# A decoder trunk's first projection fed by quarters of x from two DMA queues, and its last norm taken by halves

## The chip, the cores and the metric

The kernel runs on one core of one Trainium2 chip. The metric is device time in microseconds (us) for one execution. Engines are named as in the profile: PE is TensorE, PEld its weight loads, DVE is VectorE, ACT ScalarE, POOL GpSimd, SP SyncE, which issues DMAs. A name with a q behind it (SPq) is that engine's instruction queue.

## What is computed

Two decoder layers over 256 tokens of width 1024, in float32, and a final norm:

```
def _layer(x, ...):
    proj = _rmsnorm(x, g_mix) @ w_in                       # 7244 columns
    (qa, ka, va, qb, kb, vb, fl, qc, kc, vc, qi, ki, wi, gl) = split(proj)
    br_a = stick_breaking_attention(qa, ka, va)
    br_b = forgetting_attention(qb, kb, vb, cumsum of log_sigmoid(fl + b_forget))
    br_c = indexed_sparse_attention(rope(qc), rope(kc), vc, rope(qi), rope(ki), wi, top 64)
    y = sum over b of sigmoid(gate_b) * (br_b @ w_branch[b])
    x = x + y @ w_out
    return x + square(relu(_rmsnorm(x, g_mlp) @ w_up)) @ w_down

def reference(x, ...):
    for layer in range(2): x = _layer(x, ...)
    return _rmsnorm(x, g_final)        # x * rsqrt(mean(x * x) + 1e-6) * g_final
```

## The kernel before

Every matrix product keeps float32 accuracy with three matmuls in a shorter format: each operand is held as a high and a low part, and `mm3` (L117) adds high x high (L119), high x low (L120) and low x high (L121). Weights come from memory as `raw` tiles, four row tiles of 128 rows at a time; `split` (L84) makes the high part on ACT (`whi`, L91) and the low part on DVE (`wlo`, L92). There are four `raw` buffers and four of each part.

`norm_in` (L157) brings x into the form that the projection needs. x is held as two row blocks (j) of 128 tokens and two halves (h) of 512 columns. For each pair of 128-column blocks its `part` transposes four 128x128 pieces on PE (`xtp`, L168), writes the high part on ACT (`xTh`, L173) and the low part on DVE (`xTl`, L174), scaled by the layer's gain `gT`. For each half it squares x on ACT with a running sum (L178). The factor of the norm (`rstd_of`, three steps on POOL, L185 to L188) is applied only when a product is evacuated.

The head of the kernel is the first layer's projection of 1100 columns: `stream_groups` (L207) takes two column groups together, 364 columns into banks `mm` and 368 into banks `at`. The order is row tiles 0 to 3 of the first group, 0 to 3 of the second, then 4 to 7 of each. A tile is two matmul triples, one for each row block. Each finished group is evacuated by ACT (`ct`, L239). A third group of 368 columns follows. Before it, SP loads x in three pieces (two of 128 x 512, then the second half as one), the gains, and four row tiles of the first group one by one; every DMA is issued by SP. A scheduler orders each engine's instructions by its own estimate of their times; only PE keeps the written order, and only in one later place.

The tail is the last layer's down projection into two halves of 512 columns (cg), the second half with row block 0 finished before row block 1. For each row block DVE adds the product to x (L713), ACT squares it with a running sum (L716), DVE multiplies by the final gain (L717), POOL makes the factor (L185, L186, L188), ACT and DVE rescale one half each (L723, L725), and SP issues each half (L724, L726).

Of the kernel before, what the change touches and what calls it, by code (L numbers as in the profile page):

```python
# [9 lines left out]
F32 = mybir.dt.float32  # L10
# [11 lines left out]
EPS = 1e-6  # L22
# [10 lines left out]
def trunk_kernel(ctx: ExitStack, tc: tile.TileContext, x, positions, g_mix, w_in, b_forget, w_branch,  # L33
# [25 lines left out]
    gload = const.tile([16, 128], F32, name="gload", tag="gload")  # L59

    def load_x(h):
        dma.dma_start(xh[h], AP(x, h * 512, [[D, 128], [128 * D, 2], [1, 512]]))
# [11 lines left out]
    def g_cols(src, c):  # L74
        p = at_tile("gps")
        pe.transpose(p[:, 0:16], src, ident[0:16, 0:16])
        dve.tensor_copy(gT[:, c:c + 16], p[:, 0:16])

    g_cols(gload, 0)
# [4 lines left out]
    def split(raw, k, n, steps=1):  # L84
# [4 lines left out]
        m = k // steps  # L89
        for i in range(0, k, m):  # L90
            act.activation(h3[:, i:i + m], raw[:, i:i + m], AF.Copy)  # L91
            dve.tensor_sub(l3[:, i:i + m], raw[:, i:i + m], h3[:, i:i + m].bitcast(F32))  # L92
        return h3, l3
# [5 lines left out]
    def w_rows(src, off, rs, k0, n, loads=1):  # L99

        raw = raw_tile(4, n)
        m = 4 // loads
        for i in range(0, 4, m):
            dma.dma_start(raw[:, i:i + m, :], AP(src, off + (k0 + i) * 128 * rs, [[rs, 128], [128 * rs, m], [1, n]]))
        r = []
        for q in range(2):
            h, l = split(raw[:, 2 * q:2 * q + 2, :], 2, n, 2 if loads == 4 and q == 0 else 1)
            r += [(h[:, i, :], l[:, i, :]) for i in range(2)]
        return r

# [46 lines left out]
    def norm_in(gcol, banks):  # L157
# [4 lines left out]
        def part(h):  # L162
            for kp in range(2):
# [5 lines left out]
                for i in range(2):  # L169
# [3 lines left out]
                    act.activation(hi, p[:, i * 256:i * 256 + 256], AF.Copy, scale=g)  # L173
                    dve.scalar_tensor_tensor(lo, p[:, i * 256:i * 256 + 256], g, hi.bitcast(F32),  # L174
                                             op0=OP.mult, op1=OP.subtract)
            for j in range(2):
# [38 lines left out]
    for layer in range(DEPTH):  # L215
        wi0 = layer * D * COLS
        if layer == 0:
            wfirst = w_rows(w_in, C0 + 736, COLS, 0, 364, loads=4)
            load_x(1)
            xt, ss, part = norm_in(0, (at_tile, pt_tile))  # L220
            part(0)
            part(1)
        rstd = rstd_of(ss)
        with tc.tile_pool(name=f"att{layer}", bufs=1, reuse_waits="tile") as att:
            work = att

            rp = at_tile("rp")
            for j in range(2):
                pe.transpose(rp[:, j * 128:j * 128 + 128], rstd[:, j:j + 1].to_broadcast([128, 128]), ident)
            rb = small.tile([128, 272], F32, name="rb", tag="rb", bufs=1)[:, 0:256]  # L230
            act.activation(rb, rp[:, 0:256], AF.Copy)

            rhalf = small.tile([128, 2], F32, name="rhalf", tag="rhalf", bufs=1)
            pool.tensor_scalar(rhalf, rstd, 0.5, 1.0, op0=OP.mult, op1=OP.mult)
# [6 lines left out]
            cgs = [(736, 364), (0, 368)]  # L241
            stream_groups(xt, 8, w_in, [(wi0 + C0 + c, n) for c, n in cgs], COLS,
                          done=lambda g, o: ct_done(*cgs[g], o), first=wfirst if layer == 0 else None)
            ct_done(368, 368, stream_tok(xt, 8, w_in, wi0 + C0 + 368, COLS, 368))

            if layer == 0:
                gload2 = const.tile([16, 128], F32, name="gload2", tag="gload")
                dma.dma_start(gload2, AP(g_mlp, 0, [[128, 16], [1, 128]]))
# [58 lines left out]
                g_cols(gload2, 16)  # L307
# [357 lines left out]
        with tc.tile_pool(name=f"mlp{layer}", bufs=1, reuse_waits="tile") as mlp:  # L665
# [38 lines left out]
            if last:  # L704
                gfb = mlp.tile([128, D], F32, name="gfb")
                dma.dma_start(gfb, AP(g_final, 0, [[0, 128], [1, D]]))
                ss = small.tile([128, 2, 2], F32, name="ss")
            else:
                xt, ss, part = norm_in(layer * 8 + 8, (at_tile, pt_tile))
            for cg in range(2):  # L710
                o = stream_tok(uT, 32, w_down, layer * DFF * D + cg * 512, D, 512, split_last=last and cg == 1)
                for j in range(2):
                    dve.scalar_tensor_tensor(xs[j][cg], o[j], r2[:, j:j + 1], xs[j][cg], op0=OP.mult, op1=OP.add)  # L713
                    if last:
                        junk = small.tile([128, 512], mybir.dt.bfloat16, name="junk", tag="junk", bufs=1)
                        act.activation(junk, xs[j][cg], AF.Square, accum_out=ss[:, j, cg:cg + 1])  # L716
                        dve.tensor_mul(xs[j][cg], xs[j][cg], gfb[:, cg * 512:cg * 512 + 512])  # L717
                if not last:
                    part(cg)
                for j in range(2):  # L720
                    if last and cg == 1:
                        rl = rstd_of(ss[:, j:j + 1, :])
                        act.activation(xs[j][1], xs[j][1], AF.Copy, scale=rl)  # L723
                        dma.dma_start(AP(out, j * 128 * D + 512, [[D, 128], [1, 512]]), xs[j][1])  # L724
# [25 lines left out]
```

## Time and profile before

| | us |
|---|---|
| median of three runs | 889.51 (888.76 to 890.77) |
| the profiled execution | 889.98 |
| its span, first to last instruction | 888.3 |
| PE busy | 873.0 (98%) |
| DVE busy | 621.6 (70%) |
| ACT busy | 531.1 (60%) |
| POOL busy | 113.9 (13%) |

The span is what the trace covers; the rest of an execution's time lies around it. Shares are of the whole span, so they don't tell where PE stands still. The chain that ended last gives 92% of the span to PE, 4% to DVE, and 1% each to ACT, DMA and issue.

### The profile page before, as it was taken

How to read it: one execution, taken by the hardware profiler on the slowest of the kernel's cores; microseconds unless marked ns; L12 is line 12 of the kernel's file. 1: busy time of each engine (PE TensorE's matmuls, PEld its weight loads, DVE VectorE, ACT ScalarE, POOL GpSimd, SP SyncE). 2: the span in 40 equal slices, each digit the busy share in tenths (PEclk: the TensorE clock that was granted, in tenths of full speed). 3: DMA queues.
4: the chain of work that ended last, by engine and by line, in shares of the span. 5: the costliest groups of instructions: out<-in, count | busy, mean ns of one | idle time of the engine just before them, and what ended most of it. 6: DMA issues, size and time to landing. Idle time of an engine off the chain costs nothing.

```text
span 888.3 us, 13911 instructions
## 1 busy us (share of the span) xinstructions
PE 873.0 (98%) x5342; PEld 789.1 (89%) x5342; DVE 621.6 (70%) x1008; ACT 531.1 (60%) x874; POOL 113.9 (13%) x216
## 2 busy tenths in 40 slices
PE   7999999999999999999999999999999999999996
PEld 7998998888889999888899989988888999998885
DVE  5899787978766666545468987789876676664552
ACT  6766886776455555444365758677755655553442
POOL 2300321234001000000011014022600100000001
PEclk9999999999999999999999999999999999999998
DMA  8744544354555555555466463453346555555521
GB/s 288 244 147 143 190 143 143 116 169 143 190 190 164 176 183 190 190 189 190 137 208 195 139 197 136 143 189 128 106 150 232 169 190 190 190 188 192 190 95 48
DMA packets 102482, 150.97 MB, mean 170 GB/s; under 512 B 2928, under 2 KB 58256, under 8 KB 102416
## 3 DMA queue, kind: packets, MB, share of 16 engines
q1 hardware_dynamic: 102416, 150.08, 51.5%
q8 instruction: 42, 0.69, 0.3%
q14 instruction: 24, 0.20, 0.1%
HBM read 149.02 MB, written 1.05 MB: 169 GB/s over the span
## 4 chain that ended last, share of the span: by engine, by line
PE 92%; DVE 4%; ACT 1%; DMA 1%; issue 1%; SPq 0%; POOL 0%; POOLq 0%; ACTq 0%
PE mm L120 26%; PE mm L119 26%; PE mm L121 26%; PE av L454 2%; PE pT L438 2%; PE at L120 1%; PE at L121 1%; PE at L119 1%; DVE wlo L92 1%; DVE qs L145 1%; PE xtp L168 1%; ACT qs L143 1%; DMA x<-in_x_dram 1%; PE za L347 0%; PE yTp L579 0%
## 5 line engine op out<-in xcount | busy, mean ns | idle before, releaser
L92 DVE TENSOR_TENSOR wlo<-raw,whi 128x1024 fp32r<-128x1024 f32 (+3 forms) x289 | 347.8, 1206 | 201.0 <-ACT whi L91 199.4
L91 ACT ACTIVATE whi<-raw 128x1024 fp32r<-128x1024 f32 (+3 forms) x289 | 298.5, 1036 | 253.1 <-PE mm L121 142.4
L121 PE MATMUL mm<-xTh,wlo 128*128 128x256 f32 x752 | 214.0, 285 | 0.0
L119 PE MATMUL mm<-xTh,whi 128*128 128x256 f32 x752 | 213.8, 284 | 0.0
L120 PE MATMUL mm<-xTl,whi 128*128 128x256 f32 x752 | 213.6, 284 | 0.0
L119 PEld LDWEIGHTS mm<-xTh,whi 128*128 128x128 f32 x752 | 144.2, 192 | 0.2
L120 PEld LDWEIGHTS mm<-xTl,whi 128*128 128x128 f32 x752 | 144.2, 192 | 0.2
L121 PEld LDWEIGHTS mm<-xTh,wlo 128*128 128x128 f32 x752 | 144.2, 192 | 0.0
L120 PE MATMUL mm<-wlo,xTh 128*128 128x512 f32 (+2 forms) x320 | 122.7, 384 | 0.5 <-DVE wlo L92 0.5
L121 PE MATMUL mm<-whi,xTl 128*128 128x512 f32 (+2 forms) x320 | 121.6, 383 | 0.0
L119 PE MATMUL mm<-whi,xTh 128*128 128x512 f32 (+2 forms) x320 | 119.4, 383 | 0.3 <-ACT xTh L173 0.3
L121 PE MATMUL mm<-whi,ul 128*128 128x512 f32 x256 | 99.7, 389 | 0.0
L120 PE MATMUL mm<-wlo,uh 128*128 128x512 f32 x256 | 99.6, 389 | 0.0
L119 PE MATMUL mm<-whi,uh 128*128 128x512 f32 x256 | 99.2, 389 | 0.0
L120 PEld LDWEIGHTS mm<-wlo,xTh 128*128 128x128 f32 x320 | 61.0, 191 | 10.3 <-DVE wlo L92 1.3
L119 PEld LDWEIGHTS mm<-whi,xTh 128*128 128x128 f32 x320 | 60.9, 190 | 10.2 <-ACT xTh L173 0.7
L121 PEld LDWEIGHTS mm<-whi,xTl 128*128 128x128 f32 x320 | 60.8, 190 | 9.0
L185 POOL TENSOR_TENSOR ms<-ss 128x2 f32<-128x2 f32 (+1 forms) x6 | 4.3, 718 | 474.4 <-ACT junk L178 297.7
L121 PEld LDWEIGHTS mm<-whi,ul 128*128 128x128 f32 x256 | 48.1, 188 | 10.0
L120 PEld LDWEIGHTS mm<-wlo,uh 128*128 128x128 f32 x256 | 48.1, 188 | 10.0
L119 PEld LDWEIGHTS mm<-whi,uh 128*128 128x128 f32 x256 | 48.1, 188 | 9.7
L487 POOL TENSOR_SCALAR e<-e,rs 128x128 f32<-128x128 f32 x64 | 43.2, 693 | 27.2 <-DVE rs L484 27.2
(215 smaller groups left out, 1274.0 us busy)
## 6 DMA issues: line engine op xcount, KB each, us to landing
raw<-in_w_in_dram SPq DMA_DIRECT2D x48, 1024.0 KB, 5.0
raw<-in_w_up_dram SPq DMA_DIRECT2D x32, 1024.0 KB, 5.1
raw<-in_w_down_dram SPq DMA_DIRECT2D x32, 1024.0 KB, 5.0
raw<-in_w_branch_dram SPq DMA_DIRECT2D x12, 1024.0 KB, 5.0
raw<-in_w_out_dram SPq DMA_DIRECT2D x8, 1024.0 KB, 5.0
raw<-in_w_in_dram SPq DMA_DIRECT2D x8, 736.0 KB, 5.4
raw<-in_w_in_dram SPq DMA_DIRECT2D x3, 728.0 KB, 4.3
out_dram<-x SPq DMA_DIRECT2D x4, 256.0 KB, 2.2
```

The costliest lines, as they stand in the source:

```text
L91: act.activation(h3[:, i:i + m], raw[:, i:i + m], AF.Copy)
L92: dve.tensor_sub(l3[:, i:i + m], raw[:, i:i + m], h3[:, i:i + m].bitcast(F32))
L119: pe.matmul(o, ah, bh, start=start, stop=False)
L120: pe.matmul(o, ah, bl, start=False, stop=False)
L121: pe.matmul(o, al, bh, start=False, stop=stop)
L143: act.activation(dst[half(i), :, i, :], src[half(i)], AF.Copy, scale=scale)
L145: dve.scalar_tensor_tensor(dst[half(1 - i), :, i, :], src[half(i)], scale, dst[half(i), :, i, :].bitcast(F32), op0=OP.mult, op1=OP.subtract)
L168: pe.transpose(p[:, i * 256 + j * 128:i * 256 + j * 128 + 128], xs[j][h][:, c:c + 128], ident)
L185: pool.tensor_add(ms, ss[:, :, 0], ss[:, :, 1])
L438: pe.transpose(p[:, q * 128:q * 128 + 128], e[:, i, q * 128:q * 128 + 128], ident)
L454: pe.matmul(o[:, c + c0:c + 256], v, p[:, a:b], start=s == 0 and n == 0, stop=s == 1 and n == 1)
L487: pool.tensor_scalar(e[:, i, c:c + n], e[:, i, c:c + n], rs[:, i, j:j + 1], 1.0, op0=OP.mult, op1=OP.mult)
```

## The change

x is loaded by quarters: 256 columns of both row blocks each. ACT issues four of the first DMAs (the gains, two row tiles, one quarter), SP the others. The first four row tiles of both column groups are loaded by `head_rows` in single tiles (the last two of the second group in one), and each is split just before the previous tile's matmuls are written. The quarters' transposes are written between the matmuls of the first two groups (`head_mid`), the squares of a half by themselves. PE, ACT and DVE keep the written order from the first instruction to the sine table's steps behind the second group (`tc.manual_schedule`; the scheduler fits later work in between); within it a group's weights are split when its turn comes, and `ct_done` follows its last matmul. The transposes of the norm row (`rp`) move to the last row tiles of the second group.

At the end, the gain is scaled by 32 once it is loaded, so that the mean's 1/1024 goes and the factor is one power on POOL. The last half is added and squared in two halves of 256 columns, the sums are added in one DVE operation, all squares are written ahead of the rescales, ACT issues the outputs that it rescales, and ACT, DVE and POOL keep the written order.

```diff
-    for j in range(2):
-        dma.dma_start(xh[0][:, j, :], AP(x, j * 128 * D, [[D, 128], [1, 512]]))
-    dma.dma_start(gload, AP(g_mix, 0, [[128, 16], [1, 128]]))
+    def load_x(queue, q):
+        queue.dma_start(xh[q // 2][:, :, (q % 2) * 256:(q % 2) * 256 + 256],
+                        AP(x, q * 256, [[D, 128], [128 * D, 2], [1, 256]]))
+    act.dma_start(gload[0:16], AP(g_mix, 0, [[128, 16], [1, 128]]))
+    load_x(dma, 0)
...
+    def head_rows(off, n):
+        raw = raw_tile(4, n)
+        two = {}
+        def load(queue, i, m=1):
+            queue.dma_start(raw[:, i:i + m, :], AP(w_in, off + i * 128 * COLS, [[COLS, 128], [128 * COLS, m], [1, n]]))
+        def part(i):
+            if i % 2 == 0:
+                two[i // 2] = [wp.tile([128, 1024], F32R, name=t, tag=t, bufs=4) for t in ("whi", "wlo")]
+            h, l = [t[:, i % 2 * n:i % 2 * n + n] for t in two[i // 2]]
+            act.activation(h, raw[:, i], AF.Copy)
+            dve.tensor_sub(l, raw[:, i], h.bitcast(F32))
+            return h, l
+        return load, [lambda i=i: part(i) for i in range(4)]
...
-                ws = first if first and not (k0 or g) else w_rows(src, off, rs, k0, n)
+                ws = list(first[g]) if first and not k0 else w_rows(src, off, rs, k0, n)
...
+                    if callable(ws[i]):
+                        ws[i] = ws[i]()
                     if mid is not None:
                         mid(k0, g, q)
+                    if i < 3 and callable(ws[i + 1]):
+                        ws[i + 1] = ws[i + 1]()
...
-            wfirst = w_rows(w_in, C0 + 736, COLS, 0, 364, loads=4)
-            load_x(1)
-            xt, ss, part = norm_in(0, (at_tile, pt_tile))
-            part(0)
-            part(1)
-        rstd = rstd_of(ss)
+            load0(act, 0)
+            load0(dma, 1)
+            load_x(act, 1)
+            load0(dma, 2)
+            load0(act, 3)
+            load1(dma, 0)
+            load1(dma, 1)
+            load_x(dma, 2)
+            load1(dma, 2, 2)
+            load_x(dma, 3)
+            xt, ss, part = norm_in(0, (pt_tile, pt_tile))
+            order = tc.manual_schedule(engines={mybir.EngineType.PE, mybir.EngineType.Activation, mybir.EngineType.DVE})
+            order.__enter__()
+            warm = small.tile([128, 2], F32, name="ms")
+            act.activation(warm, mhalf, AF.Square)
+            g_cols(0, 0)
+            part(0, (0,), False)
...
+            def head_mid(k0, g, q):
+                if (k0, g, q) == (0, 0, 2):
+                    part(0, (1,), False)
+                if (k0, g, q) == (0, 1, 4):
+                    part(1, (0,), False)
+                if (k0, g, q) == (0, 1, 6):
+                    part(1, (1,), False)
+                if (k0, g, q) == (0, 1, 2):
+                    part(0, ())
+                if (k0, g, q) == (0, 1, 7):
+                    part(1, ())
+                    norms()
+                if (k0, g, q) == (4, 1, 4):
+                    norm_row()
...
+                act.activation(gfb, gfb, AF.Copy, scale=32.0)
...
+                    steps = 2 if cg else 1
+                    n = 512 // steps
+                    for h in range(steps):
+                        xv = xs[j][cg][:, h * n:h * n + n]
+                        dve.scalar_tensor_tensor(xv, o[j][:, h * n:h * n + n], r2[:, j:j + 1], xv, op0=OP.mult, op1=OP.add)
...
+                        act.activation(junk[:, :n], xv, AF.Square, accum_out=fs[:, j, cg + h:cg + h + 1])
...
+                        if j:
+                            rescale(0, 1)
+                        dve.tensor_scalar(ms[:, j:j + 1], fs[:, j, 1:2], fs[:, j, 0:1], fs[:, j, 2:3], op0=OP.add, op1=OP.add)
+                        pool.tensor_tensor(rl[:, j:j + 1], ms[:, j:j + 1], mhalf[:, 0:1], op=OP.pow)
+                    dve.tensor_mul(xs[j][cg], xs[j][cg], gfb[:, cg * 512:cg * 512 + 512])
+                if cg:
+                    rescale(0, 0)
+                    rescale(1, 0)
+                    rescale(1, 1)
```

Here `rescale(j, 1)` is a DVE product whose output SP issues, and `rescale(j, 0)` an ACT product whose output ACT issues.

ACT in the head, kernel before. `junk` is a square of x, `xTh` an evacuation of transposed x, `whi` a split (364 or 728 columns belong to the first column group, 368 or 736 to the second and third), `ct` the evacuation of a column group, `rb` the norm row, `trig` the sine table.

```order
L178 ACTIVATE junk,ss<-x_71 128x512 x2
L173 ACTIVATE xTh<-xtp,gT 128x256 x2
L91 ACTIVATE whi<-raw 128x736 x2
L173 ACTIVATE xTh<-xtp,gT 128x256 x2
L91 ACTIVATE whi<-raw 128x728 x2
L231 ACTIVATE rb<-rp 128x256
L173 ACTIVATE xTh<-xtp,gT 128x256
L91 ACTIVATE whi<-raw 128x736 x3
L239 ACTIVATE ct<-mm,rstd 128x364 x2
L91 ACTIVATE whi<-raw 128x736
L302 ACT_TABLE_LOAD
```

The same engine and place now, from the last row tile of the first four:

```order
L119 ACTIVATE whi<-raw 128x368
L187 ACTIVATE xTh<-xtp,gT 128x256 x2
L196 ACTIVATE junk,ss<-x_71 128x512 x2
L89 ACTIVATE whi<-raw 128x728 x2
L303 ACTIVATE ct<-mm,rstd 128x364 x2
L89 ACTIVATE whi<-raw 128x736 x5
L279 ACTIVATE rb<-rp 128x256
L303 ACTIVATE ct<-at,rstd 128x368 x2
L336 ACTIVATE sel<-self 128x8
```

The splits of the second group's row tiles 4 to 7 (736 columns) stood ahead of the first group's evacuation and now stand behind it; the squares of the second half stood ahead of its evacuations and now stand between these and the first group's split.

DVE in the tail, kernel before: the accumulates (L713), the gain products (L717), the rescales (L725).

```order
L713 SCALAR_TENSOR_TENSOR x_71<-mm,r_8606,x_71 128x512
L717 TENSOR_TENSOR x_71<-x_71,gfb 128x512
L725 TENSOR_SCALAR x_70<-x_70,rstd 128x512
L713 SCALAR_TENSOR_TENSOR x_71<-mm,r_8606,x_71 128x512
L717 TENSOR_TENSOR x_71<-x_71,gfb 128x512
L725 TENSOR_SCALAR x_70<-x_70,rstd 128x512
```

DVE in the tail now, with the sum of the squares as `fms`:

```order
L802 SCALAR_TENSOR_TENSOR x_71<-mm,r_8619,x_71 128x256 x2
L810 TENSOR_SCALAR fms<-fs 128x1
L812 TENSOR_TENSOR x_71<-x_71,gfb 128x512
L802 SCALAR_TENSOR_TENSOR x_71<-mm,r_8619,x_71 128x256 x2
L791 TENSOR_SCALAR x_71<-x_71,frstd 128x512
L810 TENSOR_SCALAR fms<-fs 128x1
L812 TENSOR_TENSOR x_71<-x_71,gfb 128x512
L791 TENSOR_SCALAR x_71<-x_71,frstd 128x512
```

Row block 0's rescale stood ahead of row block 1's accumulate and now stands behind it; each gain product follows directly on the sum that POOL's power waits for.

## Rows read from the trace of the kernel before

**Rows 1.** Table of stretches: length, busy PE, PEld, DVE, ACT, POOL, clock, DMA

```profile
16.00:36.00 20.00, 20.00 (x122) 19.97 (x121) 13.77 (x39) 14.38 (x21) 2.90 (x7) 1.00 0.81 257
...
50.00:877.00 827.00, 825.86 (x5057) 743.95 (x5056) 583.52 (x924) 494.51 (x809) 98.74 (x166) 1.00 0.51 166
```

**Rows 2.** Timeline of PE, head: start, duration, engine, line, operation, tiles

```profile
4.96 1.97 PE L168 MATMUL xtp<-ident,x 128*128 128x128 f32 x8
...
7.21 0.67 PE L119 MATMUL mm<-whi,xTh 128*128 128x364 f32 x1 [0.28 <-ACT xTh L173]
...
7.68 0.51 PE L120 MATMUL mm<-wlo,xTh 128*128 128x364 f32 x1
...
10.08 1.97 PE L168 MATMUL xtp<-ident,x 128*128 128x128 f32 x8 [0.68 <-DMA x<-in_x_dram]
...
15.11 0.33 PE L121 MATMUL mm<-whi,xTl 128*128 128x364 f32 x1
...
20.68 0.33 PE L121 MATMUL at<-whi,xTl 128*128 128x368 f32 x1
...
36.80 0.66 PE L326 MATMUL ctT<-ident,ct 128*128 128x128 f32 x4
```

**Rows 3.** Chain that ended last, head: start, duration, what

```profile
13.26 0.61 PE mm L121 x2
```

**Rows 4.** Timeline of ACT, head

```profile
5.79 1.01 ACT L91 ACTIVATE whi<-raw 128x364 fp32r<-128x364 f32 x2 [0.55 <-DMA raw<-in_w_in_dram]
...
8.53 0.82 ACT L173 ACTIVATE xTh<-xtp,gT 128x256 fp32r<-128x256 f32 x2
...
14.34 0.82 ACT L91 ACTIVATE whi<-raw 128x728 fp32r<-128x728 f32 x1
...
24.28 1.02 ACT L239 ACTIVATE ct<-mm,rstd 128x364 f32<-128x364 f32 x2 [0.73 <-PE mm L121]
...
26.02 1.28 ACT L302 ACT_TABLE_LOAD   x1
```

**Rows 5.** Timeline of DVE, head

```profile
6.33 1.04 DVE L92 TENSOR_TENSOR wlo<-raw,whi 128x364 fp32r<-128x364 f32 x2 [1.09 <-ACT whi L91]
...
8.66 0.92 DVE L92 TENSOR_TENSOR wlo<-raw,whi 128x728 fp32r<-128x728 f32 x1 [0.90 <-ACT whi L91]
```

**Rows 6.** DMA issues by tile: count, KB each, median us to landing

```profile
raw<-in_w_in_dram SPq DMA_DIRECT2D x4, 182.0 KB, 3.8
x<-in_x_dram SPq DMA_DIRECT2D x2, 256.0 KB, 2.9
...
gload<-in_g_mix_dram SPq DMA_DIRECT2D x1, 8.0 KB, 3.0
```

**Rows 7.** Chain that ended last, tail

```profile
877.22 0.76 DVE x L713
...
878.81 0.71 POOL ms L185
...
881.70 0.73 ACT junk L716 x2
...
883.29 0.19 POOL ms L186
...
883.52 0.61 POOLq L746
...
884.15 0.72 ACT x L723
```

**Rows 8.** Timeline, tail

```profile
878.76 0.69 DVE L717 TENSOR_TENSOR x<-x,gfb 128x512 f32<-128x512 f32 x1 [0.79 <-ACT junk L716]
...
879.51 0.39 PE L121 MATMUL mm<-whi,ul 128*128 128x512 f32 x1
...
885.04 0.43 SPq L724 DMA_DIRECT2D out_dram<-x  x1
```

**Rows 9.** Table of stretches behind the last matmul

```profile
882.00:883.00 1.00, 0.00 (x0) 0.00 (x0) 0.54 (x1) 0.42 (x2) 0.50 (x1) 0.50 1.02 385
```

More of the change, by code (lines that the diff above doesn't have):

```diff
@@ L88, in split @@
         l3 = lo[:, :k * n].rearrange("p (k n) -> p k n", k=k)
[L89 to L92, printed above, removed]
+        act.activation(h3, raw, AF.Copy)
+        dve.tensor_sub(l3, raw, h3.bitcast(F32))
         return h3, l3
@@ L160, in norm_in, with part @@
         ss = small.tile([128, 2, 2], F32, name="ss")
-        def part(h):
-            for kp in range(2):
+        def part(h, kps=(0, 1), squares=True):
+            for kp in kps:
                 p = banks[h]("xtp")
@@ L224, in trunk_kernel @@
         with tc.tile_pool(name=f"att{layer}", bufs=1, reuse_waits="tile") as att:
             work = att
[L227 to L233, printed above, removed]
@@ L234, in trunk_kernel, with norms, norm_row @@
-            pool.tensor_scalar(rhalf, rstd, 0.5, 1.0, op0=OP.mult, op1=OP.mult)
+            def norms():
+                nonlocal rstd, rhalf
+                rstd = rstd_of(ss)
+                rhalf = small.tile([128, 2], F32, name="rhalf", tag="rhalf", bufs=1)
+                pool.tensor_scalar(rhalf, rstd, 0.5, 1.0, op0=OP.mult, op1=OP.mult)
+            def norm_row():
+                nonlocal rb
+                rp = pt_tile("rp")
+                for j in range(2):
+                    pe.transpose(rp[:, j * 128:j * 128 + 128], rstd[:, j:j + 1].to_broadcast([128, 128]), ident)
+                rb = small.tile([128, 272], F32, name="rb", tag="rb", bufs=1)[:, 0:256]
+                act.activation(rb, rp[:, 0:256], AF.Copy)
@@ L236, in trunk_kernel @@
+            if layer:
+                norms()
+                norm_row()
             ct = att.tile([128, 2, 1152], F32, name="ct", tag="G", bufs=1)[:, :, 0:CN]
@@ L239, in ct_done @@
                     act.activation(ct[:, j, c0:c0 + n], o[j][:, :n], AF.Copy, scale=rstd[:, j:j + 1])
-            cgs = [(736, 364), (0, 368)]
             stream_groups(xt, 8, w_in, [(wi0 + C0 + c, n) for c, n in cgs], COLS,
-                          done=lambda g, o: ct_done(*cgs[g], o), first=wfirst if layer == 0 else None)
-            ct_done(368, 368, stream_tok(xt, 8, w_in, wi0 + C0 + 368, COLS, 368))
+                          done=lambda g, o: ct_done(*cgs[g], o), first=None if layer else [h for _, h in head],
+                          mid=None if layer else head_mid)
             if layer == 0:
-                gload2 = const.tile([16, 128], F32, name="gload2", tag="gload")
-                dma.dma_start(gload2, AP(g_mlp, 0, [[128, 16], [1, 128]]))
+                dma.dma_start(gload[32:48], AP(g_mlp, 0, [[128, 16], [1, 128]]))
                 pos = const.tile([128, 2], I32, name="pos")
@@ L706, in trunk_kernel @@
                 dma.dma_start(gfb, AP(g_final, 0, [[0, 128], [1, D]]))
[L707 removed]
+                act.activation(gfb, gfb, AF.Copy, scale=32.0)
+                fs = mlp.tile([128, 2, 4], F32, name="fs")
+                ms = mlp.tile([128, 2], F32, name="fms")
+                rl = mlp.tile([128, 2], F32, name="frstd")
             else:
@@ L718, in trunk_kernel @@
[L718 to L724, printed above, removed]
-                        dve.tensor_scalar(xs[j][0], xs[j][0], rl, None, op0=OP.mult)
-                        dma.dma_start(AP(out, j * 128 * D, [[D, 128], [1, 512]]), xs[j][0])
+                if not last:
+                    for j in range(2):
+                        dve.scalar_tensor_tensor(xs[j][cg], o[j], r2[:, j:j + 1], xs[j][cg], op0=OP.mult, op1=OP.add)
+                    part(cg)
+                    continue
@@ new lines, in trunk_kernel, with rescale @@
+                if cg:
+                    end = tc.manual_schedule(engines={mybir.EngineType.Activation, mybir.EngineType.DVE, mybir.EngineType.Pool})
+                    end.__enter__()
+                def rescale(j, c):
+                    if c:
+                        dve.tensor_scalar(xs[j][1], xs[j][1], rl[:, j:j + 1], None, op0=OP.mult)
+                        dma.dma_start(AP(out, j * 128 * D + 512, [[D, 128], [1, 512]]), xs[j][1])
+                    else:
+                        act.activation(xs[j][0], xs[j][0], AF.Copy, scale=rl[:, j:j + 1])
+                        act.dma_start(AP(out, j * 128 * D, [[D, 128], [1, 512]]), xs[j][0])
```

42 lines of the change are left out of this document (24 added, 18 removed).

## The prediction

> **What bounds the kernel now.** I read the table of stretches first [rows 1]: from 50 to 877 us TensorE (PE) is busy 825.86 of 827.00 us, and from 16 to 36 us all of the time. So nothing can be won between the ends; what is there to win lies in the first 16 us and behind the last matmul, and any new wait of PE inside the full stretches is paid in full. The row of 16 to 36 us prices a matmul of 364 or 368 columns, which nearly all are: 122 in 20.00 us, 0.164 us each.
>
> The head, by PE's own timeline [rows 2]: eight transposes of x from 4.96, first matmul at 7.21, its second at 7.68, then the other half of x holds it until 10.08. A matmul lasts 0.51 us there and 0.33 from 15.11 on; two of them take 0.61 in the chain [rows 3], so 0.305 each. The one is the 1.2 GHz level, the other the 2.4. PE ran from 10.08 without a gap before that change. By 20.68 + 0.165 = 20.85 it has done row tiles 0 to 3 of both first column groups (48 matmuls), two more matmuls and two transposes for the norm row; without these the 48 would be done at about 20.3. That moment is what I compare.
>
> The tail, by the chain of waits [rows 7]: the last accumulate, the square, three Pool steps, the rescale, the output. PE's last matmul ends at 879.51 + 0.39 = 879.90, and the last output is issued at 885.04 [rows 8]: 5.14 us.
>
> **The change part by part.**
>
> *Start.* The gains' load goes first on ScalarE's (ACT's) queue, a quarter of x first on SP's. With 3.0 and 2.9 us to landing [rows 6] and an issue at 0.8 both are there at 3.8 (before, the gains were issued third, behind both row blocks of x). One small transpose (0.25, estimated from a full one) and four of 1.97 / 8 = 0.246 us [rows 2] end at 5.05; two evacuations on ACT (0.82 for two), one split (1.01 / 2 = 0.5) [rows 4], and 0.2 of hand-over give the first matmul at 6.6; the split's VectorE (DVE) half (1.04 / 2 = 0.52) [rows 5] gives the second at 7.2, where it was at 7.68. If the quarter lands late this shifts: bounds from the rows are 2.9 us and the 3.8 us of the weight loads beside it [rows 6], so up to +0.9. The warm-up activation and the table load (1.28, [rows 4]) on ACT end at about 4.1, before the first transposes, and cost nothing; the four DMA issues ahead of them are priced by SP's, 0.43 each [rows 8].
>
> The Trainium skill (DMA: Bandwidth & Descriptors, "Issuing engines are not separate DMA queues") says that copies issued by different engines run on the same 16 DMA engines and interleave, and save only issue time. By that the quarter shares the engines with ACT's loads and would land towards the late bound; the sum would be 0.9 higher. No run here shows two queues yet.
>
> *From there to the 48th matmul.* Five matmuls 1.5 (8.8), four transposes 1.0 (9.8). The clock: before, it rose 5 us after PE's last gap; I take the same distance, 12.2, with bounds 10 and 15. Until then some 7 matmuls (0.3 us goes on the third row tile, whose split stands behind the second quarter's evacuation), then 11 x 0.165 (14.0), 12 x 0.165 (16.0), four transposes 0.45, six matmuls 1.0, four transposes (17.9). The fourth row tile of the second group waits again: its split is behind the third quarter's evacuations (16.45 + 0.2 + 0.82 + 0.5 + 0.52 = 18.5), 0.7 us; six matmuls later it is 19.7. **Term 1: 19.7 - 20.3 = -0.6 us** (-1.2 to +1.2 with both bounds).
>
> *Stall A.* The order of ACT is now written by hand. Behind the last quarter's transposes stand two evacuations, both squares of the second half, and only then the split of row tiles 4 and 5. From 17.9: 0.2 + 0.82 to 19.0, two squares of 0.73 [rows 7] to 20.5, 0.82 for the 728-column split [rows 4] to 21.3, 0.92 on DVE [rows 5] to 22.2. PE is ready at 19.7; it waits 1.6 us for the high part, does one matmul, and waits 0.8 for the low part. Before, the scheduler had put this split at 14.34, two microseconds ahead of need. **Term 2: +2.4** (1.5 to 3.0: if the evacuation starts before the fourth transpose ends, or the squares hold).
>
> *Stall B.* Next in ACT's order are the two evacuations of the first column group, which wait for PE's end of that group, and behind them the splits of the second group's row tiles 4 to 7. So PE ends the group at 22.3 + 23 x 0.165 = 26.1; the first evacuation may start 0.4 earlier, two take 1.02 [rows 4], the split 0.82, its DVE half 0.92. PE waits 1.6, does one matmul, waits 0.8. Before, these splits stood ahead of the evacuation at 24.28. **Term 3: +2.4** (1.5 to 3.0). Nothing covers this chain: it begins with PE's own last matmul of the group.
>
> *Behind the head.* The sine table's load was at 26.02 [rows 4], 10.8 us ahead of the indexer's transposes at 36.80 [rows 2], which hang on it through the rotary steps. Now it stands behind the second group's evacuation and one more split: stall B ends at 28.6, 24 matmuls and the norm row's two transposes 4.2 (32.8), evacuations 1.1, split 0.82, small steps, so at about 35.5. Table and sine 1.5, six rotary steps on Pool some 3, a DVE split of 1024 columns in front of the key copies: the first copy is done at 41.4. PE comes there at 36.8 + 4.2 = 41.0. I find it waiting 0.6 us for the copies and 1.0 soon after for a bank that DVE frees late; these small steps are estimates from their neighbours. **Term 4: +1.6** (0 to 2.5; below nothing is excluded, as PE has no idle there to give back).
>
> *Middle.* The six transposes moved at each layer's end can wait 0.3 us each; the scaling of the final gain is one ACT operation of 1024 columns while ACT is idle between splits. Cost 0 (0 to 0.6).
>
> *Tail.* DVE's accumulate of a half takes about 0.42 (half of 0.76 [rows 7] and some start), from 879.94: halves at 880.4 and 880.8. The squares follow each half: 0.45 each, to 881.3, and the sum on DVE to 881.55. So the first Pool step (0.71) and the second (0.19) go, and the accumulate no longer stands behind row block 0's rescale. Then Pool's power (0.61) and DVE's gain product (0.69 [rows 8]) are released together. If they run side by side the factor is there at 882.2; the trace shows Pool's sum of one column taking 0.71 beside exactly such a product and ending with it, while the next Pool step on one column takes 0.19 [rows 7, 8]. So I let the power's last 0.4 follow the product: 882.7. The rescale on ACT (0.72) ends at 883.45, the last issue stands at 883.6. **Term 5: 883.6 - 885.04 = -1.4 us** (-2.0 side by side; -0.9 if the power starts only behind the product and ACT's issue costs as much again as SP's 0.4).
>
> The Trainium skill (SBUF — State Buffer, "Who interferes with whom") says that a VectorE operation with two SBUF inputs keeps GpSimd from reading SBUF until it ends. The trace agrees (0.71 against 0.19 us). By the rule alone the tail wins 1.4, without it 2.0.
>
> *Sum.* -0.6 + 2.4 + 2.4 + 1.6 - 1.4 = +4.4 us. The profiled execution took 889.98 us for a span of 888.3; that would become 894.4 and 892.7. It lies 0.47 above the median of the runs, so on the median's scale 889.51 + 4.4 = 893.9: **893.9 us**.
>
> **The rivals.**
>
> *The clock falls in a stall.* After its last matmul at 879.90 PE's granted clock is 0.50 in the stretch from 882 on [rows 9], so 2.1 us without work, or less, were enough. Stalls A and B hold 2.4 us each, with one matmul inside. A fall makes the next 24 matmuls cost 0.305 instead of 0.165, 3.4 us at the most; one fall, partly, gives about 896, two 898 and more. Against it: the one matmul, and that the head's gap of 0.7 us proves nothing.
>
> *The stalls are not there (faster).* If the splits of row tiles 4 and 5 were under way by 18.0, terms 2 and 3 would go, and with them most of term 4: 889.5 - 0.6 - 1.4 = 887.5. This turns on one point: whether ACT begins its 728-column split before PE ends its 48th matmul. For it speaks that DMA has the data long before; against it, that ACT takes its instructions in the order written and that the four before it hang on PE's own last transposes.
>
> *Half of it.* Both waits shorten to about 1 us each and the key transposes do not wait: 889.5 - 0.6 + 2 - 1.4 = 889.5, no change. It needs evacuations that start after the first pair of four transposes and squares half as long; the rows speak against the second.
>
> *A late start.* The quarter lands at 4.7 and the clock rises at 15: term 1 is +1.2, and the time 895.7.
>
> **How the numbers follow.** The forecast with its own range (892 to 895.4): 0.52. Clock falls: 0.22. Late start: 0.10. Half: 0.08, nearly all of it within the bound. No stalls: 0.08. The range from 890.6 to 897.6 leaves out the faster rival and the two-fold fall. About 0.2% (1.8 us) is what a measurement of this kernel tells from no change. Faster than 887.7: 0.09; within: 0.07; slower than 891.3: 0.84.
>
> **What would show it.** In the profile after: PE's waits for ACT's and DVE's split of a weight tile, near 20 and near 26 us, of 2.4 us each; between 4 and 18 us no wait above 1 us but the start; ACT's two squares directly ahead of its first 728-column split; the last output issued 3.7 us behind PE's last matmul. The forecast is wrong if PE is busy throughout 16 to 36 us, or if the tail keeps its 5.1 us.

## The result, and the profile after

| | before | after |
|---|---|---|
| time, median of four runs each, us | 889.13 (887.38 to 890.77) | 896.38 (896.22 to 896.49) |
| ratio, 95% interval | | 1.0082, 1.0062 to 1.0101 |
| span of the profiled execution, us | 888.3 | 894.7 |
| PE's last matmul begins, us | 879.51 | 887.04 |
| from its end to the last output issue, us | 5.14 | 3.77 |

The change makes the kernel 7.25 us slower. The tail gives 1.4 us back; everything else is lost ahead of it: PE's last matmul begins 7.53 us later, and 5.97 of these are gone by 43 us.

PE's timeline of the head after; the bracket is the idle time ahead of the instruction and what released it. Before, PE had no such wait between 15 and 62 us, and its stretch from 16 to 36 us was full [rows 1].

```profile
18.84 0.44 PE L134 MATMUL at<-wlo,xTh 128*128 128x368 f32 x1 [0.52 <-DVE wlo L120]
...
20.98 0.44 PE L133 MATMUL mm<-whi,xTh 128*128 128x364 f32 x1 [1.03 <-ACT whi L89]
...
21.93 0.51 PE L134 MATMUL mm<-wlo,xTh 128*128 128x364 f32 x1 [0.51 <-DVE wlo L90]
...
28.95 0.43 PE L133 MATMUL at<-whi,xTh 128*128 128x368 f32 x1 [1.38 <-ACT whi L89]
...
29.91 0.43 PE L134 MATMUL at<-wlo,xTh 128*128 128x368 f32 x1 [0.53 <-DVE wlo L90]
...
42.35 0.34 PE L135 MATMUL mm<-whi,xTl 128*128 128x368 f32 x1
...
51.11 0.30 PE L405 MATMUL kT<-ident,kdup 128*128 128x128 f32 x1 [0.69 <-DVE qs L159]
```

The end of the third projection's matmuls before:

```profile
36.38 0.33 PE L121 MATMUL mm<-whi,xTl 128*128 128x368 f32 x1
```

Behind a single wait at 18.84 there are two pairs of waits, each for a high part by ACT, then one matmul, then for the low part by DVE. The row at 42.35 is the same matmul as the one at 36.38 before, so 5.97 us are gone by here, 0.25 of them for a transpose of the gains that now runs ahead of this row and before ran behind it, at 36.64. One more wait follows, at 51.11.

ACT's timeline around the two pairs:

```profile
18.03 0.84 ACT L187 ACTIVATE xTh<-xtp,gT 128x256 fp32r<-128x256 f32 x2 [0.20 <-PE xtp L182]
18.75 0.63 ACT L196 ACTIVATE junk<-x 128x512 bf16<-128x512 f32 x1
19.28 0.20 ACT L196 ACTIVATION_READ_ACCUMULATOR junk<-x 128x1 f32 x1
19.51 0.63 ACT L196 ACTIVATE junk<-x 128x512 bf16<-128x512 f32 x1
20.04 0.19 ACT L196 ACTIVATION_READ_ACCUMULATOR junk<-x 128x1 f32 x1
20.14 1.49 ACT L89 ACTIVATE whi<-raw 128x728 fp32r<-128x728 f32 x2
27.18 1.02 ACT L303 ACTIVATE ct<-mm,rstd 128x364 f32<-128x364 f32 x2 [5.55 <-PE mm L135]
28.09 2.93 ACT L89 ACTIVATE whi<-raw 128x736 fp32r<-128x736 f32 x4
```

Two evacuations, two squares, then the split that PE needs; later two evacuations of the result, then the next splits. Ahead of those ACT stands idle for 5.55 us, with the splits behind the instruction that it waits in.

The table of stretches, PE only: length, busy time and instructions (those that reach in or out are counted too), granted clock, DMA share, GB/s.

```profile
20.00:21.00 1.00, 0.02 (x1) 1.00 0.68 174
21.00:22.00 1.00, 0.49 (x2) 1.00 1.05 400
22.00:23.00 1.00, 1.00 (x4) 0.57 0.43 159
23.00:24.00 1.00, 1.00 (x5) 0.50 0.22 43
24.00:25.00 1.00, 1.00 (x5) 0.50 0.86 219
25.00:26.00 1.00, 1.00 (x6) 0.72 1.06 365
26.00:27.00 1.00, 1.00 (x8) 1.00 1.07 380
...
30.00:31.00 1.00, 1.00 (x6) 1.00 0.00 0
```

After the first stall the granted clock is 0.50, the lower level (1.2 GHz), for some 3 us in which PE is fully busy but counts five or six matmuls in a stretch instead of eight: their starts lie 0.305 us apart instead of 0.167. The last of the 24 matmuls of that turn begins at 27.25; with all at the upper level, as e11 below has them, it would begin at 25.69: 1.6 us. The second stall is no shorter (2.3 us against 2.0, from the end of the matmul ahead and without the one inside), and 1.00 follows it.

The tail's timeline after, row block 1 (junk is the square, fms the sum, frstd the power):

```profile
889.12 0.27 DVE L810 TENSOR_SCALAR fms<-fs 128x1 f32<-128x1 f32 x1 [0.39 <-ACT junk L804]
889.32 0.68 DVE L812 TENSOR_TENSOR x<-x,gfb 128x512 f32<-128x512 f32 x1
889.48 0.93 POOL L811 TENSOR_TENSOR frstd<-fms,mhalf 128x1 f32<-128x1 f32 x1 [1.84 <-DVE fms L810]
...
890.45 0.72 ACT L794 ACTIVATE x<-x,frstd 128x512 f32<-128x512 f32 x1 [0.74 <-POOL frstd L811]
...
891.20 0.35 ACTq L795 DMA_DIRECT2D out_dram<-x  x1
```

The power of row block 1 in the kernel before:

```profile
883.56 0.56 POOL L188 TENSOR_TENSOR rstd<-ms,mhalf 128x1 f32<-128x1 f32 x1
```

The two Pool steps ahead of the power [rows 7] are gone; the power itself takes 0.93 us beside the gain product and ends 0.41 behind it. In the kernel before, with DVE idle beside it, it took 0.56.

### The profile page after: what moved, and what is told of

Same layout as the page of the kernel before. It is cut to its first block, busy times and chain, and to the rows that moved or that the text cites. A ratio compares the mean times of both kernels' runs of the same rounds, so it can differ in the third digit from the quotient of the medians.

```text
span 894.7 us, 13946 instructions
## 1 busy us (share of the span) xinstructions
PE 876.2 (98%) x5342; PEld 789.6 (88%) x5342; DVE 621.5 (69%) x1017; ACT 531.1 (59%) x883; POOL 109.7 (12%) x212
## 4 chain that ended last, share of the span: by engine, by line
PE 89%; DVE 5%; ACT 1%; issue 1%; POOLq 0%; POOL 0%; ACTq 0%
PE mm L134 25%; PE mm L133 25%; PE mm L135 25%; PE av L518 2%; PE pT L502 2%; DVE wlo L90 1%; PE at L134 1%; PE at L135 1%; PE at L133 1%; DVE qs L159 1%; PE xtp L182 1%; ACT qs L157 0%; PE za L411 0%; PE yTp L643 0%; PE za L412 0%
## 5 line engine op out<-in xcount | busy, mean ns | idle before, releaser
L90 DVE TENSOR_TENSOR wlo<-raw,whi 128x1024 fp32r<-128x1024 f32 (+2 forms) x284 | 344.3, 1215 | 200.8 <-ACT whi L89 199.2
L89 ACT ACTIVATE whi<-raw 128x1024 fp32r<-128x1024 f32 (+2 forms) x284 | 294.5, 1042 | 247.8 <-PE mm L135 137.9
L134 PEld LDWEIGHTS mm<-wlo,xTh 128*128 128x128 f32 x320 | 61.3, 192 | 12.3 <-DVE wlo L90 2.2
```

What stands on the lines that cost most here:

```text
L89: act.activation(h3, raw, AF.Copy)
L90: dve.tensor_sub(l3, raw, h3.bitcast(F32))
L134: pe.matmul(o, ah, bl, start=False, stop=False)
```

## The experiments

All times are medians of 5 to 11 runs (the changed kernel's of four), and "d" is the difference to the median of the kernel before, run beside them. That median itself moved: 888.94 for e1 to e4, 889.39 for e5 to e8, 889.19 for e9 to e11 and 889.38 for e12. So runs with different medians of the kernel before are compared by d. The intervals reach 0.8 to 1.3 us to each side (the changed kernel's 1.7); a step of less than 1 us in d is therefore settled only where the traces show it too.

| run | us | d, us | ratio, 95% interval |
|---|---|---|---|
| changed kernel | 896.38 | +7.25 | 1.0062 to 1.0101 |
| e1 new tail alone | 888.30 | -0.64 | 0.9984 to 1.0001 |
| e2 squares later | 895.26 | +6.32 | 1.0054 to 1.0079 |
| e3 second group's splits earlier | 892.33 | +3.39 | 1.0033 to 1.0061 |
| e4 both, evacuations later too | 890.74 | +1.80 | 1.0014 to 1.0033 |
| e5 = e4 with the old tail | 892.52 | +3.13 | 1.0026 to 1.0052 |
| e6 = e4, third projection first | 890.52 | +1.13 | 1.0009 to 1.0027 |
| e7 = e4, old order in later norms | 890.49 | +1.10 | 1.0008 to 1.0026 |
| e8 = e4 + e6 + e7 + last splits earlier | 888.63 | -0.76 | 0.9986 to 1.0004 |
| e9 = e8, first group's splits earlier | 888.40 | -0.79 | 0.9987 to 1.0005 |
| e10 = e9 with one queue | 888.09 | -1.10 | 0.9981 to 0.9999 |
| e11 changed kernel, PE kept busy | 895.09 | +5.90 | 1.0059 to 1.0084 |
| e12 = e10, pairs, positions first | 887.57 | -1.81 | 0.9974 to 0.9992 |

**e1, the tail alone.** The kernel before, with the last norm's branch exchanged for the changed kernel's:

```
-                        dve.scalar_tensor_tensor(xs[j][cg], o[j], ...)
...
-                        rl = rstd_of(ss[:, j:j + 1, :])
...
+                    for h in range(steps):
+                        dve.scalar_tensor_tensor(xv, o[j][:, h * n:h * n + n], ...)
...
+                    rescale(0, 0)
+                    rescale(1, 0)
+                    rescale(1, 1)
```

> The kernel before with the new last norm alone (halves, all squares ahead of the rescales, outputs issued by two engines); its head is untouched. Theory: the loss sits in the head's order and the tail gains what the trace shows, 1.4 us from PE's last matmul to the last output issue, so about 887.8 us, 1.3 below before. Rival: the end is set by the outputs' landing, not by their issue, and the tail gives nothing: 889.1. Rival: the new tail itself pays for part of the loss: 890 or more.

Measured -0.64 us, with an interval that just holds zero. In its trace PE's last matmul begins at 879.40 and the last output is issued at 883.55, 3.76 us behind its end as in the changed kernel, so the step is there. The runs of the kernel before spread over 2.6 us and those of e1 over 2.2, which blurs it; with the same tail and another head, e4's spread over 0.7, and e5 measures the tail there. The tail is no part of the loss.

**e2, the squares behind the splits.**

```
-                if (k0, g, q) == (0, 1, 7):
+                if (k0, g, q) == (4, 0, 0):
                     part(1, ())
                     norms()
```

> The changed kernel with one move: the squares and the norm of the second half of x are written behind the splits of row tiles 4 to 7 instead of ahead of them. Theory: ACT's order makes PE wait, and that wait brings the clock down: of the 2.0 us of waits at the 49th matmul about 0.6 stay (the split itself), the 1.6 us at the low clock go, so about 893.4 us, 3 below the changed kernel. Rival: the clock falls there whatever the order, about 895.0. Rival: the squares only go late and the evacuations of the result wait for the norm instead: 896.4, no change.

PE's timeline in e2, its waits behind 20 us:

```profile
20.71 0.43 PE L134 MATMUL mm<-wlo,xTh 128*128 128x364 f32 x1 [0.54 <-DVE wlo L90]
...
26.17 0.43 PE L133 MATMUL at<-whi,xTh 128*128 128x368 f32 x1 [1.38 <-ACT whi L89]
...
27.13 0.44 PE L134 MATMUL at<-wlo,xTh 128*128 128x368 f32 x1 [0.53 <-DVE wlo L90]
```

And its table of stretches, columns as above:

```profile
21.00:22.00 1.00, 1.00 (x8) 1.00 1.05 393
...
27.00:28.00 1.00, 0.87 (x4) 0.83 0.00 0
28.00:29.00 1.00, 1.00 (x5) 0.50 0.09 6
29.00:30.00 1.00, 1.00 (x5) 0.50 0.80 179
30.00:31.00 1.00, 1.00 (x6) 0.50 1.08 381
```

The first stall shrinks to the low part's 0.54 us and the clock does not fall behind it: half of the theory. But now it falls behind the second stall, which is as it was. So the price of the fall moved instead of going, and d went down by 0.9 us where 3 were expected. The five runs lie at 893.7, 893.8 and three at 895.3: two groups 1.5 us apart, about the price of one fall. Only a run of the upper group (895.26) has a trace; that the lower ones had no fall is not shown.

**e3, the second group's splits ahead of the first group's evacuations.** In the loop over matmuls, with `w_rows` called early and its result used when the group begins:

```
+                    if first and (k0, g, q) == (4, 0, 2):
+                        ahead = w_rows(src, groups[1][0], rs, 4, groups[1][1])
```

> The changed kernel with one move: the splits of row tiles 4 to 7 of the second column group are written behind those of the first group, ahead of the evacuations of the first group's result. Theory: the second stall (2.3 us at 28.9 us) goes and nothing takes its place: 894.1 us. Rival: the evacuations come late in their turn and the third projection or the transposes behind it wait for them: 895.5 to 896.4.

PE's timeline in e3, its only waits between 19 and 40 us:

```profile
20.97 0.44 PE L133 MATMUL mm<-whi,xTh 128*128 128x364 f32 x1 [1.06 <-ACT whi L89]
...
21.92 0.44 PE L134 MATMUL mm<-wlo,xTh 128*128 128x364 f32 x1 [0.52 <-DVE wlo L90]
```

One stretch of its table:

```profile
22.00:23.00 1.00, 1.00 (x6) 1.00 0.38 143
```

The second stall is gone and nothing takes its place; d falls by 3.9 us. That is more than the stall's 2.3, because the profiled run has no fall of the clock although its first stall is the changed kernel's to 0.03 us: its stretch from 22 to 23 us counts six matmuls at 1.00 where the changed kernel counts four at 0.57. Its runs lie in two groups as well: three at 892.2 to 892.3, the traced one among them, and two at 893.3 and 893.9. A stall of this length can bring the clock down; it does not do so every time.

**e4, both moves,** and the fourth quarter's evacuations with the squares, so that ACT has only the third quarter's and one split ahead of the splits of row tiles 4 to 7. Beside e3's edit:

```
-                if (k0, g, q) == (0, 1, 6):
-                    part(1, (1,), False)
-                if (k0, g, q) == (0, 1, 7):
-                    part(1, ())
+                if (k0, g, q) == (4, 0, 0):
+                    part(1, (1,))
                     norms()
```

> Both moves together, and the last two evacuations of x behind the splits of row tiles 4 to 7 as well, so that ACT has nothing ahead of these splits. Theory: both stalls and the clock's fall go: 2.0 + 1.6 + 2.3 = 5.9 us off, 890.5 us, with the clock up from 12 us on and no wait of PE over 0.5 us between 12 and 40 us. Rival: two queues and quarters of x, not ACT's order, carry most of the loss: above 893. Rival: the earlier start is worth more than the 0.5 us seen so far once the stalls are gone: 888 or below, which beats before.

890.74, within 0.3 us of the theory, and the ten runs lie within 0.71 us of each other. PE's timeline in e4 has two waits between 12 and 45 us:

```profile
17.89 0.44 PE L133 MATMUL at<-whi,xTh 128*128 128x368 f32 x1 [0.32 <-ACT whi L119]
...
18.85 0.44 PE L134 MATMUL at<-wlo,xTh 128*128 128x368 f32 x1 [0.52 <-DVE wlo L120]
```

So 5.45 of the 7.25 us are the order of the head's splits, squares and evacuations (with the last quarter's four transposes, which move along) and what that order does to the clock. What was left, 1.8 us over the kernel before with a better tail, shows when PE's matmuls of e4 and e1 (same tail) are laid side by side, start against start: e4 is 0.39 us later in the third projection, 1.28 at 106 us, 1.60 at 280 and 1.95 from 720 us to the end. Between these steps the distance does not change by more than 0.03 us. e6 and e7 take the steps one by one.

**e5, e4 with the old tail,** the exchange of e1 the other way round.

> The version with both moves of the head (890.74 us, its runs within 0.7 us of each other) and the last norm as it was before. It measures the tail on a head that varies less than the head before. Theory: the new tail is worth the 1.4 us between PE's last matmul and the last output issue, so 892.1 us here. Rival: only the 0.7 us by which the new tail alone lowered the median, 891.4. Rival: nothing, 890.7.

d rises by 1.33 us (3.13 - 1.80); in the traces the last output is issued 5.15 us behind PE's last matmul here and 3.77 in e4. The tail is worth what its trace says. The medians alone differ by 1.78: in the runs of e5 to e8 the kernel before is 0.45 us slower as well, and in their four traces the first matmul begins between 6.45 and 6.69 us, where it begins at 5.98 in e4.

**e6, the third projection ahead of the constants again.**

```
             if layer == 0:
+                order.__exit__(None, None, None)
+            ct_done(368, 368, stream_tok(xt, 8, w_in, wi0 + C0 + 368, COLS, 368))
+            if layer == 0:
                 dma.dma_start(gload[32:48], ...)
...
-                order.__exit__(None, None, None)
-            ct_done(368, 368, stream_tok(xt, 8, w_in, wi0 + C0 + 368, COLS, 368))
```

> The version with both moves, and the third projection written ahead of the constants again, with the order by hand ended in front of it. Theory: the key transposes wait for low parts on DVE that stand behind the constants (0.6 us of idle PE, and 0.8 us lost between 36 and 80 us against the kernel before); with the old order both go: 889.9 us. Rival: the scheduler gives them the same places, 890.7.

This row of e4's PE timeline is gone in e6:

```profile
45.09 0.30 PE L407 MATMUL kT<-ident,kdup 128*128 128x128 f32 x1 [0.58 <-DVE qs L159]
```

Side by side with e4, PE in e6 stands 0.98 us later at 36 us (its first loads landed 0.7 later in this execution), and 0.10 later from 83 us on: 0.88 us won in that stretch. d falls by 0.67. The median, 890.52, is nearer to the rival's 890.7 than to the theory's 889.9, but it lies beside the slower median of the kernel before (889.39); the wait that is gone decides for the theory.

**e7, the later norms in their old order.**

```
                     act.activation(hi, ...)
+                    if squares and len(kps) == 2:
+                        dve.scalar_tensor_tensor(lo, ...)
-                for i in range(2):
+                for i in range(2 * (len(kps) < 2)):
```

> The version with both moves, and the later norms (two in the middle) with each low evacuation behind its own high one again, instead of two high ones and then two low ones. Theory: PE loses 0.32 us at 268 and again at 702 us against the kernel before because the first low part comes one evacuation later; this goes: 890.1 us. Rival: the loss there comes from another place of the schedule, 890.7.

Eight transposes of x between two stages in the middle of the kernel, PE's timeline of e4:

```profile
267.76 1.37 PE L182 MATMUL xtp<-ident,x 128*128 128x128 f32 x8
```

The same in e7:

```profile
268.47 1.04 PE L182 MATMUL xtp<-ident,x 128*128 128x128 f32 x8
```

The distance to e4 drops by 0.32 us here and again at 702 us. The wait lies inside a group of eight: nothing shows in brackets, only the group is longer. d falls by 0.70, of which 0.64 is accounted for; the median alone (890.49) would again not tell the theory from the rival.

**e8, all of these, and the last splits earlier.**

```
+                    if first and i < 3 and callable(ws[i + 1]):
+                        ws[i + 1] = ws[i + 1]()
                     if mid is not None:
                         mid(k0, g, q)
```

> The version with both moves, the third projection and the later norms as in the two runs beside it, and the last split of each of the first two groups of row tiles written ahead of the evacuations of x that stand in front of it now. Theory: the 0.85 us that PE waits at 17.9 and 18.9 us go as well: 890.74 - 0.8 - 0.6 - 0.85 = 888.5 us, 0.4 below the kernel before. Rival: the split that comes early delays the evacuation of x behind it and PE waits there instead: 889.3.

888.63 against 888.5 expected, though e4's runs lay beside a kernel before of 888.94 and these beside 889.39; by d the step from e4 is 2.56 us, where 2.25 were expected and the traces of e4, e6 and e7 give 0.88 + 0.64 + 0.84. The terms found one by one add up within the noise. Against the kernel before e8 is not told from no change.

**e9, the first group's splits ahead of the third quarter's evacuations.**

```
+                    if first and (k0, g, q) == (0, 1, 4):
+                        rows[4, 0] = w_rows(src, groups[0][0], rs, 4, groups[0][1])
                     if mid is not None:
                         mid(k0, g, q)
```

> The best version so far (888.63 us) with the splits of row tiles 4 to 7 of the first group written ahead of the third and fourth evacuations of x. Theory: its last wait of PE in the head, 0.7 us at 19.7 us for a low split that stood behind two low parts of x on DVE, goes, and ACT uses the 2.0 us that it waited there for the transposes: 887.8 us, below the kernel before by about 1. Rival: these rows land only at about 16 us, the evacuations of x come late in their turn, and PE waits for those: 888.6.

The theory fails: d does not move (-0.79 against -0.76). PE's only wait in e8 between 8 and 60 us:

```profile
19.73 0.43 PE L134 MATMUL mm<-wlo,xTh 128*128 128x364 f32 x1 [0.69 <-DVE wlo L90]
```

Its two in e9:

```profile
18.97 0.43 PE L135 MATMUL mm<-whi,xTl 128*128 128x364 f32 x1 [0.52 <-DVE xTl L195]
...
23.48 0.43 PE L134 MATMUL at<-wlo,xTh 128*128 128x368 f32 x1 [0.42 <-DVE wlo L90]
```

The wait for the low split has gone, and waits for a low part of x and for another split have come. What stands in the way is a cast on DVE that waits for a load (2.07 us here); its rows are shown for e10.

**e10, one queue.** Beside e9:

```
-    act.dma_start(gload[0:16], ...)
+    dma.dma_start(gload[0:16], ...)
-            load0(act, 0)
-            load_x(act, 1)
-            load0(act, 3)
+            load0(dma, 0)
+            load_x(dma, 1)
+            load0(dma, 3)
```

> The same as the run beside it, but with every load of the head issued by SP's queue alone, in the same order. It asks what the second queue is worth. Theory: three more issues stand ahead on SP at 0.6 us each, x's second quarter and the first row tiles land up to 1.8 us later, and PE, which waits for the first split at 6.5 us, starts 0.6 to 1.8 us later; part of it comes back since the clock rises some microseconds after PE starts and so later: plus 0.5 to 1.8 us on the run beside it. Rival: PE's beginning is hidden by the transfers (two queues share the same engines), no change.

No slower: -1.10 against -0.79, so the theory of 0.5 to 1.8 us more is wrong. PE's first matmul begins at 6.31 against 6.12 us, and ACT loads its table at 0.78 instead of 2.77 us. The Trainium skill (DMA: Bandwidth & Descriptors, "Issuing engines are not separate DMA queues"), by which a second queue saves issue time alone, agrees: 0.19 us at the first matmul is all that is seen of it. DVE's timeline in e10:

```profile
14.29 0.54 DVE L120 TENSOR_TENSOR wlo<-raw,whi 128x368 fp32r<-128x368 f32 x1 [0.69 <-ACT whi L119]
16.52 0.17 DVE L356 CAST posf<-pos 128x2 f32<-128x2 int32 x1 [1.69 <-DMA pos<-in_positions_dram]
...
16.94 0.91 DVE L90 TENSOR_TENSOR wlo<-raw,whi 128x728 fp32r<-128x728 f32 x1
...
18.95 0.87 DVE L195 SCALAR_TENSOR_TENSOR xTl<-xtp,gT,xTh 128x256 fp32r<-128x256 f32 x2
```

A cast of two columns waits 1.69 us for the positions, with the splits and the low part of x that PE needs behind it; PE waits 0.84 us for that low part at 19.48.

**e11, the stalls as they are, PE busy.** In the changed kernel, at the start of both stalls, twelve transposes that nobody reads:

```
+                if (k0, q) == (4, 0):
+                    p = pt_tile("fill")
+                    for f in range(12):
+                        pe.transpose(p[:, 0:128], xs[0][0][:, 0:128], ident)
```

> The changed kernel, its order untouched, with twelve transposes of x into an unused bank (read by nobody) on PE at the start of each of the two stalls. The stalls stay as long as they are; PE works in the greater part of them. Theory: the clock falls in the head because PE stands idle there, so with PE busy it stays at its upper level, the 24 matmuls behind the first stall take 4 us instead of 5.6, and the time is 896.4 - 1.6 = 894.8 us. Rival: the clock falls there whatever PE does, 896.4 us. Rival: the transposes come in the way of what follows: above 896.5.

PE's timeline in e11 at the first stall:

```profile
19.71 1.47 PE L298 MATMUL fill<-ident,x 128*128 128x128 f32 x12
20.94 0.41 PE L133 MATMUL mm<-whi,xTh 128*128 128x364 f32 x1
21.86 0.43 PE L134 MATMUL mm<-wlo,xTh 128*128 128x364 f32 x1 [0.51 <-DVE wlo L90]
22.14 0.33 PE L135 MATMUL mm<-whi,xTl 128*128 128x364 f32 x1
```

The real matmuls come as late as in the changed kernel, to 0.1 us (20.94 and 21.86 against 20.98 and 21.93), the one behind them takes 0.33 us, and every stretch from 20 to 36 us has the clock at 1.00. PE's last matmul begins 1.64 us earlier, and d is 1.35 us less. One trace would not settle it, since e3's first stall passed without a fall and without filling; but e11's five runs lie within 0.35 us at 894.8 to 895.2, and the changed kernel's four all lie at 896.2 to 896.5. So the fall comes with PE standing idle in the stall, and is worth about the 1.6 us read from the trace.

**e12, pairs, and the positions first.** Beside e10:

```
-                        rows[4, 0] = w_rows(...)
+                        pair = w_rows(..., True)
+                        rows[4, 0] = pair(0)
                     if mid is not None:
                         mid(k0, g, q)
+                    if first and (k0, g, q) == (0, 1, 4):
+                        rows[4, 0] += pair(1)
...
+    act.dma_start(pos, AP(positions, 0, [[1, 128], [128, 2]]))
```

The last line stands at the start of the kernel, the load's old place is empty.

> The one-queue version (888.09 us) with two moves: the second split of row tiles 4 to 7 stands behind the third evacuation of x and the first ahead of it, and the positions are loaded first on ACT's queue. Theory: in the one-queue version DVE stands from 14.8 to 16.5 us in a constant that waits for the positions, with two low splits and a low part of x behind it, and PE waits 0.84 us for that low part at 19.5 us; this goes, 887.2 us, below the kernel before by about 1.5. Rival: the positions land late and hold up DVE's first low parts at 5 us, and PE's start with them: 888 to 889.

887.57: faster than the kernel before by 0.7 to 2.3 us by the ratio's interval, and about 1% faster than the changed kernel. Behind its second matmul at 7.60 us PE has no wait in its rows up to 60 us, and DVE's cast of the positions stands at 2.99 us without a wait. What each of the two moves is worth was not measured.

## Why the prediction came out as it did

- *Direction and mechanism: right.* Slower, by waits of PE for ACT's and DVE's splits at the two places named, with the head's earlier start too small to pay for them. e4 shows it: undoing the order takes 5.45 of 7.25 us away.
- *Term 1, -0.6:* the 48th matmul ends at 19.79, -0.5 against 20.3. The first matmul came at 6.14 (6.6 expected): x's first quarter was there by 3.56 us, so the late bound of +0.9 was not touched. The matmuls reach 0.33 us at 12.3 (12.2 expected), which is luck: in e2, e3 and e11, whose heads are alike up to the first stall, they reach it at 10.4 to 10.7. The 48th matmul ends within 0.15 us of the same time there, because the waits that follow take up the difference.
- *Term 2, +2.4:* the two waits of the first stall hold 2.0 us from the 48th matmul's end, the squares directly ahead of the split as described. *Term 3, +2.4:* 2.3, at 29 us instead of 26.
- *The clock.* This is the step that was mis-sized. The sum held both stalls at the upper level and left the fall to a rival with a chance of 0.22 and about 896 us. It happened behind the first stall and cost 1.6 us, so 896.38 lies above the forecast's own 892 to 895.4, at that rival's number. The argument against it, the one matmul inside a stall, does not hold; nor does its opposite, since e3 had the same stall without a fall. What decides between the two no run shows. That the time meets the rival's about 896 so well is in part luck, since terms 2, 4 and the middle missed in both directions.
- *Term 4, +1.6:* too large. PE waits once, 0.69 us, and e6 wins 0.67 to 0.88.
- *Middle, 0 (0 to 0.6):* 0.64, just above the upper bound. The price of 0.3 us was right and the place was not. I had named the six transposes at each layer's end, where PE's distance to the kernel before grows by only 0.07 us (400 to 500 us); the 0.64 comes from the eight transposes of x in the middle of each layer (1.37 against 1.04 us, twice). `part` now writes both high evacuations ahead of both low ones in every norm, which I had not listed among the changes.
- *Tail, -1.4:* -1.37 in the trace, 1.33 by e5. The rest of the power behind the product was the term that decided it: 0.41 us, expected 0.4. The rule of the Trainium skill that the prediction names (SBUF — State Buffer, "Who interferes with whom") goes with that: 0.93 us beside the product, 0.56 alone.
- *Sum.* Expected +4.4. The terms by the trace: -0.5 + 2.0 + 1.6 + 2.3 + 0.9 + 0.64 - 1.37 = +5.6. PE's last matmul moved by 7.53 and the last issue by 6.16; the 0.6 us between lie in pieces of 0.3 and less around the stalls and up to 106 us, and I can't put them to rows. From the last issue to the span's end it takes 3.24 us before and 3.49 after. The two profiled executions differ by 6.43 and the medians by 7.25, since the execution of the kernel before (889.98) is 0.85 above the median of its four runs.

## What to carry to other kernels

An order written by hand puts the waits of an engine in front of everything behind them: for each evacuation, square or cast that waits for PE or a transfer, ask which split PE needs next and whether it stands behind it. A stall of two microseconds on PE may cost nearly twice its length (here 2.0 and 1.6 us), since the clock may fall behind it, so price it at both. Where a kernel is left 1 us too slow with no wait to be seen, lay the starts of its matmuls beside those of the other kernel: the steps in the distance give the places.

## What the runs showed of the hardware

- The moment at which the head's matmuls go from 0.51 to 0.33 us lies anywhere from 9.9 to 15.1 us in the fourteen profiled executions, with the first matmul between 5.95 and 7.21. With heads alike up to the first stall it is 12.3 in the changed kernel and 10.4 to 10.7 in e2, e3 and e11. The granted clock is given as 1.00 all through that time, yet 0.51 us is the length that matmuls of this width have at a granted 0.50 behind the changed kernel's first stall; so in a head the level is read from the matmuls' lengths.
- The same stall (20.97 to 21.92 in e3, 20.98 to 21.93 in the changed kernel) was once followed by the clock at 1.00 and once by 0.50.
- A second queue for this head's loads brought nothing that the times show (888.40 us with two in e9, 888.09 with one in e10).
